# Latent up projection of a hybrid encoder layer: rotary parts of two neighbouring token tiles in one instruction each

## Chip, cores and metric

One core of a Trainium2 chip runs the whole layer. The metric is device microseconds (us) of one execution; the times given are medians of several runs. A profile is one further execution, recorded instruction by instruction. TensorE is called PE in the profile, VectorE DVE, ScalarE ACT, GpSimd POOL, and the queue that issues DMAs SP.

## The reference, cut to what matters

The layer has 1024 tokens of width 1024. After a modulated RMSNorm and an input projection it attends in two groups of eight heads: chunked attention (CA) and multi-head latent attention (MLA). Then come the output projection, and a gated feed-forward part. The change lies in the part that makes queries and keys of MLA out of the latents:

```python
q = jnp.dot(rmsnorm(q_lat, g_q_latent), w_q_up).reshape(B, S, 8, 96)
kv = jnp.dot(rmsnorm(kv_lat, g_kv_latent), w_kv_up).reshape(B, S, 8, 128)
k_nope, v = kv[..., :64], kv[..., 64:]
k = jnp.concatenate([k_nope, broadcast(k_rope[:, :, None, :], 8 heads)], axis=-1)
q = rmsnorm(q, g_mla_q); k = rmsnorm(k, g_mla_k)          # over the 96 numbers of a head
q = concat(q[..., :64], rope(q[..., 64:], positions))
k = concat(k[..., :64], rope(k[..., 64:], positions))
# rope(x): x1, x2 = the two halves of 16;  [x1*cos - x2*sin, x2*cos + x1*sin]
```

Each of a head's 96 numbers is thus 64 plain ones and 32 rotary ones. The rotary part of a key is the same for all eight heads, but for the factor that the norm puts on it.

## The kernel before, in words

Tokens are laid on the 128 partitions: eight token tiles of 128. Matrix products are made in three passes of fp32 values split into a high and a low part (`gemm3`, L154 to L156). Attention runs unit by unit (one head, one half of the queries): transposed pages of queries and keys (L697, with eviction and split at L705, L706, L709 and L710), scores (L771), the row minimum (L789, L790), the exponential (L797), its scaling and splitting into two fp16 parts (L799, L800, L73 on GpSimd, L819 on VectorE), a DMA transpose by SyncE's queue (L831), and the product with the values (L859), which is evicted at L868 and L869.

The projections that a later unit needs are written as generators, the *fillers* (`f_v`, `f_qk`, `f_m`, `f_up`, `f_oca`), from which `pace` draws pieces between the attention steps, so that their matmuls fill PE's gaps. The order of the program text is not the order on the engines: the framework schedules the whole layer as a list, by a simulated timeline of its own, and writes one fixed order for each engine. An engine works its list strictly in order, and waits with all that stands behind when an operand isn't there.

`f_up(gr)` (L596 to L659) makes queries, keys and values of four MLA heads, for `gr` 0 and 1. For each of the eight token tiles `t` it runs:

- six matmuls for the queries, evicted by ACT into `rq` (L632), which is one of four buffers of tag `R`; squares (L634) and their sums by head (L637, DVE);
- three matmuls for keys and values, the keys evicted into `raw` (L643, another buffer of tag `R`), their squares and sums (L645, L646, L647);
- `rsqrt_mean` on GpSimd (L119, L120): the factors `r`, four for the query heads and four for the key heads;
- the values (L650 on ACT, L651 on DVE);
- the queries: `q_t = rq * r` for all 96 numbers (L653), then `rope_apply` on the last 32 (L654), which is four DVE instructions, two products into the space of `rq` that is free by now (L465 with the cosines, L466 with the sines) and a difference and a sum of them (L467, L468);
- the keys: the plain 64 numbers times `r` (L657), and the rotary ones out of `kr`, where `f_m` has put them, times `r` (L658).

The query and key tiles `mq` and `mk` hold two token tiles each, [128, 2, 4, 96]. Their transposes (L697) need all four token tiles of a half. `f_up(0)` must be done before the first MLA unit, and its last tiles, and all of `f_up(1)`, run beside MLA attention. GpSimd has other work in that stretch: the low parts of the weights (L84) of `f_up(1)` (`wq`, `wk`) and of the output projection (`wo`), and of the transposed outputs (`cl`).

Of the kernel before, what the change touches and what calls it, by code (L numbers as in the profile page):

```python
# [13 lines left out]
F32 = mybir.dt.float32  # L14
# [8 lines left out]
MUL, ADD, SUB, MIN, MAX = ALU.mult, ALU.add, ALU.subtract, ALU.min, ALU.max  # L23

P = 128
# [8 lines left out]
QR, KVR, ROPE, NOPE, VD = 256, 128, 32, 64, 64  # L34
QK = NOPE + ROPE
# [29 lines left out]
def layer_kernel(ctx, tc, I, out):  # L65
    nc = tc.nc
    pe, act, dve, pool, sp = nc.tensor, nc.scalar, nc.vector, nc.gpsimd, nc.sync
# [7 lines left out]
    def hi_of(eng, o, i):  # L75
        if eng == "a":
            act.activation(o, i, AF.Copy)  # L77
        elif eng == "p":
            pool.tensor_scalar(o, i, 1.0, 0.0, op0=MUL, op1=ADD)
        else:  # L80
            dve.tensor_copy(o, i)

    def lo_of(eng, o, i, hi):
        (pool if eng == "p" else dve).tensor_tensor(o, i, f32(hi), op=SUB)  # L84

    cst = ctx.enter_context(tc.tile_pool(name="cst", bufs=1))
# [30 lines left out]
    def rsqrt_mean(r, ss, n, cols=None):  # L117
        sc = ss if cols is None else ss[:, cols]
        pool.tensor_scalar(sc, sc, 1.0 / n, EPS, op0=MUL, op1=ADD)  # L119
        anchor["r"] = pool.tensor_tensor(r, ss, nhalf[:].to_broadcast(list(r.shape)), op=ALU.pow).ins  # L120
# [8 lines left out]
    tabq = apg.tile([P, NT, 64], F32, name="tabq")  # L129
    tabk = apg.tile([P, NT, 64], F32, name="tabk")  # L130
    kr = apg.tile([P, NT, ROPE], F32, name="kr")
# [9 lines left out]
    def qtile(name):  # L141
        return apg.tile([P, 512], F32, name=name, tag="sq", bufs=2)
# [134 lines left out]
    for d in range(ND):  # L277
# [8 lines left out]
        for i in range(2):  # L286
            c0 = half * 256 + i * P
# [27 lines left out]
    def pow2_scale(nm, ssw, b2, n, fac):  # L315
        t = cst.tile([P, 3, ND], F32, name=f"vs{nm}")
        dve.tensor_tensor(t[:, 0, :n], ssw, b2, op=MUL)
        pt = ps.tile([P, 512], F32, name=f"vsp{nm}", tag="mm", bufs=2)
        pe.matmul(pt[:, :n], ones[:], t[:, 0, :n], start=True, stop=True)
        dve.tensor_reduce(t[:, 1, 0:1], pt[:, :n], axis=AX.X, op=ADD)  # L320
        dve.tensor_scalar(t[:, 1, 0:1], t[:, 1, 0:1], fac, 1e-30, op0=MUL, op1=ADD)
        pool.tensor_tensor(t[:, 1, 1:2], t[:, 1, 0:1], nhalf[:], op=ALU.pow)
        ab = cst.tile([P, 2], F32, name=f"vab{nm}")
        dve.tensor_scalar(t[:, 2, 0:1].bitcast(I32), t[:, 1, 1:2].bitcast(I32), 0x7F800000, None, op0=ALU.bitwise_and)
        dve.reciprocal(t[:, 2, 1:2], t[:, 2, 0:1])
        dve.tensor_scalar(t[:, 2, 1:2], t[:, 2, 1:2], 1.0001, None, op0=MUL)
        dve.tensor_scalar(t[:, 2, 1:2].bitcast(I32), t[:, 2, 1:2].bitcast(I32), 0x7F800000, None, op0=ALU.bitwise_and)
        dve.tensor_scalar(ab[:, 0:1], t[:, 2, 0:1], VSCALE, None, op0=MUL)
        dve.tensor_scalar(ab[:, 1:2], t[:, 2, 1:2], 1.0 / (VSCALE * PSCALE), None, op0=MUL)
        return ab[:, 0:1], ab[:, 1:2]  # L330
# [128 lines left out]
    def rope_apply(o, x, tab, t, nh, tmp, eng=pool):  # L459

        a = tmp[:, 0:nh * 32].rearrange("p (a b) -> p a b", a=nh)
        b = tmp[:, nh * 32:2 * nh * 32].rearrange("p (a b) -> p a b", a=nh)
        ct = tab[:, t:t + 1, 0:32].to_broadcast([P, nh, 32])
        sn = tab[:, t:t + 1, 32:64].to_broadcast([P, nh, 32])
        eng.tensor_tensor(a, x, ct, op=MUL)  # L465
        eng.tensor_tensor(b, x, sn, op=MUL)  # L466
        eng.tensor_tensor(o[:, :, 0:16], a[:, :, 0:16], b[:, :, 16:32], op=SUB)  # L467
        eng.tensor_tensor(o[:, :, 16:32], a[:, :, 16:32], b[:, :, 0:16], op=ADD)  # L468
# [119 lines left out]
    def g4(shape, dt, name):  # L588
        return G["4"].tile(shape, dt, name=name, tag="G4", bufs=8)
# [4 lines left out]
    mq, mk, mv = {}, {}, {}  # L594

    def f_up(gr):  # L596
        if gr == 0:
            right.__exit__(None, None, None)
            for i in "4v3":
                G["cm" + i] = tc.tile_pool(name="gp" + i, bufs=1, side="right", reuse_waits="tile")  # L600
                G[i] = G["cm" + i].__enter__()
        wq = []
        for k in range(2):
            raw = qtile(f"wqr{gr}_{k}")
            sp.dma_start(raw[:, :384], I["w_qu"][gr][:, k, :])
            w = g4([P, 2, 512], F32R, f"wq{gr}_{k}")
            hi_of("a", w[:, 0, :384], raw[:, :384])
            lo_of("p", w[:, 1, :384], raw[:, :384], w[:, 0, :384])
            wq.append(w)
        raw = qtile(f"wkr{gr}")  # L610
        sp.dma_start(raw[:], I["w_kvu"][gr])
        ssw = cst.tile([P, 1], F32, name=f"sswm{gr}")
        junk = qtile(f"wkj{gr}")
        act.activation(junk[:, 0:256].rearrange("p (a b) -> p a b", a=4),
                       raw[:].rearrange("p (a b) -> p a b", a=4)[:, :, NOPE:], AF.Square, accum_out=ssw[:])
        vscale["m", gr] = pow2_scale(f"m{gr}", ssw[:], gb2[:], 1, float(KVR))
        sc = vscale["m", gr][0]
        wk = g4([P, 2, 512], F32R, f"wk{gr}")
        hi_of("a", wk[:, 0], raw[:])
        lo_of("p", wk[:, 1], raw[:], wk[:, 0])  # L620
        for t in range(NT):
            h, j = divmod(t, 4)
            sl = slice(j * P, (j + 1) * P)
            if t % 2 == 0:
                mq[gr, t // 2] = g3([P, 2, 4, QK], F32, f"qn{gr}_{t}")
                mk[gr, t // 2] = g3([P, 2, 4, QK], F32, f"kn{gr}_{t}")
                mv[gr, t // 2] = G["v"].tile([P, 2, 4, 2, 64], F16, name=f"vt{gr}_{t}", tag="Gv", bufs=8)
            pt = ps.tile([P, 512], F32, name=f"qu{gr}_{t}", tag="mm", bufs=2)
            yield from gemm3_f(pt[:, :384], [(latT[k, h][:, 0, sl], latT[k, h][:, 1, sl], wq[k][:, 0, :384], wq[k][:, 1, :384])
                                for k in range(2)])  # L630
            rq = rtile(f"uqr{gr}_{t}")
            act.activation(rq[:, :384], pt[:, :384], AF.Copy)  # L632
            sq = qtile(f"usq{gr}_{t}")
            act.activation(sq[:, :384], rq[:, :384], AF.Square)  # L634
            ss = cst.tile([P, 8], F32, name=f"uss{gr}_{t}", tag="ss", bufs=4)
            r = cst.tile([P, 8], F32, name=f"ur{gr}_{t}", tag="rr", bufs=4)
            dve.tensor_reduce(ss[:, 0:4], sq[:, :384].rearrange("p (a b) -> p a b", a=4), axis=AX.X, op=ADD)  # L637
            pt = ps.tile([P, 512], F32, name=f"ku{gr}_{t}", tag="mm", bufs=2)
            yield from gemm3_f(pt[:], [(latT[2, h][:, 0, sl], latT[2, h][:, 1, sl], wk[:, 0], wk[:, 1])])
            p4 = pt[:].rearrange("p (a b) -> p a b", a=4)  # L640
            raw = rtile(f"kraw{gr}_{t}")
            r3 = raw[:, :256].rearrange("p (a b) -> p a b", a=4)
            act.activation(r3, p4[:, :, 0:NOPE], AF.Copy)  # L643
            s3 = raw[:, 256:512].rearrange("p (a b) -> p a b", a=4)
            act.activation(s3, r3, AF.Square)  # L645
            dve.tensor_reduce(ss[:, 4:8], s3, axis=AX.X, op=ADD)  # L646
            dve.tensor_tensor(ss[:, 4:8], ss[:, 4:8], ssr[:, t:t + 1].to_broadcast([P, 4]), op=ADD)  # L647
            rsqrt_mean(r[:], ss[:], QK)
            v_t = mv[gr, t // 2][:, t % 2]
            act.activation(v_t[:, :, 0, :], p4[:, :, NOPE:], AF.Copy, scale=sc)  # L650
            dve.scalar_tensor_tensor(v_t[:, :, 1, :], p4[:, :, NOPE:], sc, v_t[:, :, 0, :], op0=MUL, op1=SUB)  # L651
            q_t = mq[gr, t // 2][:, t % 2]
            dve.tensor_tensor(q_t, rq[:, :384].rearrange("p (a b) -> p a b", a=4),  # L653
                              r[:, 0:4].unsqueeze(2).to_broadcast([P, 4, QK]), op=MUL)  # L654
            rope_apply(q_t[:, :, NOPE:], q_t[:, :, NOPE:], tabq, t, 4, rq[:, 0:256], dve)
            k_t = mk[gr, t // 2][:, t % 2]
            dve.tensor_tensor(k_t[:, :, 0:NOPE], r3, r[:, 4:8].unsqueeze(2).to_broadcast([P, 4, NOPE]), op=MUL)  # L657
            dve.tensor_tensor(k_t[:, :, NOPE:], kr[:, t:t + 1, :].to_broadcast([P, 4, ROPE]),  # L658
                              r[:, 4:8].unsqueeze(2).to_broadcast([P, 4, ROPE]), op=MUL)  # L659


    def load_wo(k0, n, he, le):
# [541 lines left out]
    c0 = mt("c", [P, 4, 512], "c0")  # L1204
# [321 lines left out]
    for t in range(4):  # L1526
        o = dl.tile([P, 512], F32, name=f"oe{t}", tag="oe", bufs=3)
# [78 lines left out]
```

## Time and profile before

| What | us |
|---|---|
| median of 3 runs | 1341.02 (1340.53 to 1343.16) |
| the profiled execution, its own time | 1345.89 |
| its span, from the first to the last instruction | 1344.1 |
| PE busy | 1223.8 (91%) |
| DVE busy | 1096.2 (82%) |
| ACT busy | 622.7 (46%) |
| POOL busy | 578.1 (43%) |

In time, the layer is: modulation and the first projections, CA attention with the projections as fillers (to about 366 us), `f_up(0)` and the start of MLA (to about 396), MLA attention with `f_up(1)` beside it (to about 490), MLA attention with the first half of the output projection as its filler (to about 620), the other half of the output projection, and the feed-forward part to the end.

A row of the timeline gives the start of an instruction, its duration, the engine, the line, the operation, its operands and, in brackets, how long the engine had been idle before it. Durations of instructions that follow each other on VectorE overlap: the next one starts before the one ahead of it ends. So what an instruction takes of the engine is read from the distance between two starts, not from its duration. In a row of the waits the first name waited for the second; then come the total in us, the times, and the longest. A row of the windows gives the length of the stretch, the busy us of PE, PEld (weight loads), DVE, ACT and POOL, each with its instructions in brackets, TensorE's granted clock, and the DMA share.

### The profile page before, as it was taken

To read this page: it belongs to the slowest core of one execution; us is meant where nothing else is said; L and a number is where in the kernel's file an instruction comes from. 1 tells how busy PE (TensorE), PEld (TensorE's weight loads), DVE (VectorE), ACT (ScalarE), POOL (GpSimd) and SP (SyncE) were. 2 spreads that over 40 slices of the span, in tenths; PEclk is the share of its full clock that TensorE was granted. 3 is DMA by queue.
4 is the path that set the end of the run, shared out by engine and by line. 5 is a ranking of instruction groups with operands and counts; after the bars stand their busy time and mean duration, and the time that the engine had idled before them with its cause. 6 is when DMAs were issued, how large, how long until landed. Compare 5 with 4: busy or idle time off the path is not lost.

```text
span 1344.1 us, 18696 instructions
## 1 busy us (share of the span) xinstructions
PE 1223.8 (91%) x6168; PEld 1003.8 (75%) x6168; DVE 1096.2 (82%) x1928; ACT 622.7 (46%) x1132; POOL 578.1 (43%) x610
## 2 busy tenths in 40 slices
PE   4899798998877798886998999999999998999998
PEld 3788587896655567765776888888888886888886
DVE  6978798864679987894989988988899997687667
ACT  4453546443555544563376444444434444433431
POOL 5464557565646763354634444444445431000000
PEclk9899798998787889996999999999999998999999
DMA  8415577854413477779911333333323326943441
GB/s 323 138 35 116 135 177 179 192 127 110 87 32 80 94 153 165 141 150 252 377 49 47 126 110 133 103 122 98 133 102 118 126 98 241 390 141 117 130 161 63
DMA packets 223689, 190.57 MB, mean 142 GB/s; under 512 B 148708, under 2 KB 166884, under 8 KB 223592
## 3 DMA queue, kind: packets, MB, share of 16 engines
q1 hardware_dynamic: 223592, 189.38, 49.1%
q8 instruction: 48, 0.79, 0.2%
q14 instruction: 49, 0.40, 0.1%
HBM read 117.24 MB, written 37.49 MB: 115 GB/s over the span
## 4 chain that ended last, share of the span: by engine, by line
PE 41%; DVE 10%; issue 3%; ACT 2%; DMA 1%; POOL 1%; SPq 0%; DVEq 0%; ACTq 0%; POOLq 0%
PE p L1082 7%; PE p L1084 7%; PE p L1083 7%; PE dnA_P L1417 2%; PE dnA_P L1419 2%; PE dnA_P L1418 2%; PE dnB_P L1419 1%; PE dnB_P L1418 1%; PE dnB_P L1417 1%; DVE u L1253 1%; DVE u L1254 1%; PE op L154 1%; PE dnA L1417 1%; PE dnA L1419 1%; PE dnA L1418 1%
## 5 line engine op out<-in xcount | busy, mean ns | idle before, releaser
L77 ACT ACTIVATE dnP<-dnr 128x1024 fp32r<-128x1024 f32 x73 | 77.5, 1064 | 117.5 <-PE dnA_P L1419 46.4
L1391 DVE TENSOR_TENSOR dnP<-dnr,dnP 128x1024 fp32r<-128x1024 f32 x72 | 87.9, 1223 | 52.6 <-ACT dnP L77 52.6
L73 POOL TENSOR_SCALAR hlm<-Pm,rim 128x512 f16<-128x512 f32 (+3 forms) x96 | 68.8, 726 | 83.5 <-DVE rim L800 22.3
L84 POOL TENSOR_TENSOR wf<-wu,wf 128x512 fp32r<-128x512 f32 x22 | 38.8, 1762 | 116.3 <-ACT wf L77 116.3
L1253 DVE SCALAR_TENSOR_TENSOR u<-c,cvp,u 128x1023 f32<-128x1023 f32 x44 | 64.8, 1513 | 27.8 <-ACT u L1252 27.8
L73 POOL TENSOR_SCALAR hlc<-Pc,ric 128x640 f16<-128x640 f32 (+2 forms) x64 | 50.8, 797 | 61.0 <-ACT Pc L797 20.8
L819 DVE SCALAR_TENSOR_TENSOR hlm<-Pm,rim,hlm 128x512 f16<-128x512 f32 (+3 forms) x96 | 68.0, 719 | 9.8 <-POOL hlm L73 9.7
L797 ACT ACTIVATE Pc<-sc,mc 128x640 f32<-128x640 f32 (+2 forms) x64 | 42.1, 658 | 53.1 <-DVE mc L786 35.9
L797 ACT ACTIVATE Pm<-sm,mm 128x128 f32<-128x128 f32 (+3 forms) x64 | 47.1, 736 | 41.7 <-DVE mm L790 24.2
L84 POOL TENSOR_TENSOR wb<-wu,wb 128x512 fp32r<-128x512 f32 x22 | 38.1, 1732 | 64.5 <-ACT wb L77 50.7
L1252 ACT ACTIVATE u<-c,cvp 128x1024 f32<-128x1024 f32 x44 | 52.3, 1237 | 27.8 <-DVE c L1351 19.2
L1254 DVE SCALAR_TENSOR_TENSOR u<-c,cvp,u 128x1022 f32<-128x1022 f32 x44 | 63.8, 1488 | 0.0
L859 PE MATMUL pvm<-PTm,vt 128*128 128x256 f16 (+1 forms) x320 | 45.7, 294 | 17.0 <-DMA PTm<-hlm 9.9
L819 DVE SCALAR_TENSOR_TENSOR hlc<-Pc,ric,hlc 128x640 f16<-128x640 f32 (+2 forms) x64 | 51.6, 809 | 9.3 <-POOL hlc L73 8.7
L155 PE MATMUL ipq<-wq_s,hT 128*128 128x256 f32 x192 | 56.0, 292 | 0.1
L859 PEld LDWEIGHTS <-vt 128*128 128x128 f16 x320 | 31.6, 109 | 32.7 <-DMA PTm<-hlm 15.0
L154 PE MATMUL ipq<-wq_s,hT 128*128 128x256 f32 x192 | 55.8, 293 | 0.0
L156 PE MATMUL ipq<-wq_s,hT 128*128 128x256 f32 x192 | 55.4, 289 | 0.0
L77 ACT ACTIVATE wc<-ws 128x512 fp32r<-128x512 f32 x21 | 13.3, 632 | 88.0 <-DVE ws L1101 82.2
L1418 PE MATMUL dnA_P<-dnP 128*128 128x512 f32 x132 | 51.4, 389 | 0.0
L1419 PE MATMUL dnA_P<-dnP 128*128 128x512 f32 x132 | 51.3, 389 | 0.0
L1417 PE MATMUL dnA_P<-dnP 128*128 128x512 f32 x132 | 51.2, 389 | 0.0
(442 smaller groups left out, 4428.4 us busy)
## 6 DMA issues: line engine op xcount, KB each, us to landing
wu<-w_up SPq DMA_DIRECT2D x44, 512.0 KB, 3.5
dnr<-g_d SPq DMA_DIRECT2D x73, 256.0 KB, 2.8
aw<-w_ada SPq DMA_DIRECT2D x48, 256.0 KB, 3.5
g_d<-u SPq DMA_DIRECT2D x22, 512.0 KB, 3.0
dnr<-w_down SPq DMA_DIRECT2D x44, 256.0 KB, 5.3
adaw<-w_ada_a SPq DMA_DIRECT2D x16, 512.0 KB, 6.3
x<-x SPq DMA_DIRECT2D x16, 512.0 KB, 9.0
g_d<-gs SPq DMA_DIRECT2D x22, 256.0 KB, 2.8
```

The costliest lines, as they stand in the source:

```text
L73: pool.tensor_scalar(o, i, s, 1.0, op0=MUL, op1=MUL)
L77: act.activation(o, i, AF.Copy)
L797: act.activation(pr[:, :n], sv, AF.Exp, bias=m[:], scale=-1.0, accum_out=rsum[:, 0:1])
L819: dve.scalar_tensor_tensor(hl[:, w:2 * w], pp, ri[:], hl[:, :w], op0=MUL, op1=SUB)
L1082: pe.matmul(pt, sh, pg[:, 0], start=(k == 0 and not add), stop=False, skip_group_check=skip)
L1083: pe.matmul(pt, sh, pg[:, 1], start=False, stop=False, skip_group_check=skip)
L1084: last = pe.matmul(pt, sl, pg[:, 0], start=False, stop=(k == 3), skip_group_check=skip)
L1253: dve.scalar_tensor_tensor(u[:, 1:], c[:, :S - 1], cvp[:, cv + 1:cv + 2], u[:, 1:], op0=MUL, op1=ADD)
L1391: r = f(*a, **k)
L1417: pe.matmul(pt, sh, w[:, 0, 0], start=start, stop=False, skip_group_check=add)
L1418: pe.matmul(pt, sh, w[:, 1, 0], start=False, stop=False, skip_group_check=add)
L1419: pe.matmul(pt, sl, w[:, 0, 0], start=False, stop=stop, skip_group_check=add)
```

## The change

The factors of two neighbouring token tiles go into one tile, `rp` [128, 2, 8], two buffers instead of four single ones. In an even token tile the rotary work is left out; in the odd one it is done for both, by instructions that are twice as long: four for the queries instead of eight, one for the keys instead of two. The products with the cosines and sines now fill all 512 columns of the odd tile's `rq`; the `rq` of the even tile is read for the last time by its `q_t`.

```diff
-            r = cst.tile([P, 8], F32, name=f"ur{gr}_{t}", tag="rr", bufs=4)
+            if t % 2 == 0:
+                rp = cst.tile([P, 2, 8], F32, name=f"ur{gr}_{t}", tag="rp", bufs=2)
+            r = rp[:, t % 2]
...
-            rsqrt_mean(r[:], ss[:], QK)
+            rsqrt_mean(r, ss[:], QK)
...
-            rope_apply(q_t[:, :, NOPE:], q_t[:, :, NOPE:], tabq, t, 4, rq[:, 0:256], dve)
+            if t % 2:
+                x = mq[gr, t // 2][:, :, :, NOPE:]
+                a = rq[:, 0:256].rearrange("p (t a b) -> p t a b", t=2, a=4)
+                b = rq[:, 256:512].rearrange("p (t a b) -> p t a b", t=2, a=4)
+                for o, c0 in ((a, 0), (b, 32)):
+                    dve.tensor_tensor(o, x, tabq[:, t - 1:t + 1, c0:c0 + 32].unsqueeze(2).to_broadcast([P, 2, 4, 32]), op=MUL)
+                dve.tensor_tensor(x[:, :, :, 0:16], a[:, :, :, 0:16], b[:, :, :, 16:32], op=SUB)
+                dve.tensor_tensor(x[:, :, :, 16:32], a[:, :, :, 16:32], b[:, :, :, 0:16], op=ADD)
             k_t = mk[gr, t // 2][:, t % 2]
             dve.tensor_tensor(k_t[:, :, 0:NOPE], r3, r[:, 4:8].unsqueeze(2).to_broadcast([P, 4, NOPE]), op=MUL)
-            dve.tensor_tensor(k_t[:, :, NOPE:], kr[:, t:t + 1, :].to_broadcast([P, 4, ROPE]),
-                              r[:, 4:8].unsqueeze(2).to_broadcast([P, 4, ROPE]), op=MUL)
+            if t % 2:
+                dve.tensor_tensor(mk[gr, t // 2][:, :, :, NOPE:], kr[:, t - 1:t + 1, :].unsqueeze(2).to_broadcast([P, 2, 4, ROPE]),
+                                  rp[:, :, 4:8].unsqueeze(3).to_broadcast([P, 2, 4, ROPE]), op=MUL)
```

The code is moved by ten lines behind the change. In the changed kernel the products of the rotary part stand at L662, the difference and sum at L663 and L664, the keys' rotary part at L668, `q_t` at L655 and the keys' plain part at L666.

## The prediction

> **What bounds the kernel now.** First the page: which engine is full. Then the windows of the stretch that holds the changed lines, then the waits in it, then VectorE's timeline.
>
> ```profile
> span 1344.1 us, 18696 instructions
> ...
> PE 1223.8 (91%) x6168; PEld 1003.8 (75%) x6168; DVE 1096.2 (82%) x1928; ACT 622.7 (46%) x1132; POOL 578.1 (43%) x610
> ```
>
> The shares are means over stages; the changed lines run in one of them only, between 376 and 490 us. By stage:
>
> ```profile
> 376.00:396.00 20.00, 15.32 (x59) 11.38 (x57) 17.63 (x58) 11.15 (x28) 10.83 (x12) 0.83 0.03 7
> 396.00:490.00 94.00, 69.14 (x326) 53.06 (x325) 87.94 (x257) 53.53 (x125) 64.39 (x64) 0.78 0.44 96
> 490.00:620.00 130.00, 113.75 (x656) 89.72 (x655) 107.65 (x268) 67.33 (x140) 59.38 (x78) 0.97 0.75 158
> ```
>
> From 396 to 490 VectorE (the third pair) is busy 87.94 of 94 us, 94%, and PE 74%: here VectorE is the bound. From 490 to 620 PE is busy 87% and VectorE 83%; they wait for each other. From 376 to 396 VectorE has 88%, and the waits say what runs there. The first three rows are of 376 to 396, the next two of VectorE from 396 to 490, the last two of VectorE from 490 to 620:
>
> ```profile
> POOL uss L119 <- DVE uss L647: 14.3, 6, 5.6
> ACT uqr L632 <- DVE kn L657: 5.6, 4, 1.8
> DVE vt L651 <- ACT vt L650: 1.1, 1, 1.1
> ```
> ```profile
> DVE vt L651 <- ACT vt L650: 1.8, 3, 0.9
> DVE mk L710 <- ACT mk L709: 1.6, 1, 1.6
> ```
> ```profile
> DVE hlm L819 <- POOL hlm L73: 8.2, 14, 1.0
> DVE sm L789 <- PE sm L771: 6.3, 10, 1.1
> ```
>
> Up to 396 it is a loop: GpSimd waits for the sum of squares, VectorE for the factors that GpSimd makes of it, ACT for a buffer that VectorE's L657 frees. A shorter VectorE instruction helps there only if it stands on that loop. From 396 to 490 VectorE's waits are small, and time taken out of its list is time gained.
>
> **The change part by part.** Five of ten rotary instructions per pair of tiles go: 5 x 8 pairs = 40 of VectorE's 1928. One tile's block, undisturbed, in the timeline:
>
> ```profile
> 378.24 0.55 DVE L653 TENSOR_TENSOR qn<-uqr,ur 128x384 f32<-128x384 f32 x1
> 378.70 0.42 DVE L657 TENSOR_TENSOR kn<-kraw,ur 128x256 f32<-128x256 f32 x1
> 379.04 0.28 DVE L658 TENSOR_TENSOR kn<-kr,ur 128x128 f32<-128x128 f32 x1
> 379.25 0.28 DVE L465 TENSOR_TENSOR uqr<-qn,tabq 128x128 f32<-128x128 f32 x1
> 379.45 0.28 DVE L466 TENSOR_TENSOR uqr<-qn,tabq 128x128 f32<-128x128 f32 x1
> 379.76 0.22 DVE L467 TENSOR_TENSOR qn<-uqr 128x64 f32<-128x64 f32 x1
> 379.91 0.22 DVE L468 TENSOR_TENSOR qn<-uqr 128x64 f32<-128x64 f32 x1
> ```
>
> From start to start, 384 columns take 0.46 us, 256 take 0.34, 128 take 0.205, 64 take 0.15: about 1 ns per column and 0.075 us for the instruction. L467 comes 0.31 behind L466 and not 0.205: it reads what L466 wrote and waits 0.11 for it. So a tile's rotary work costs 0.21 + 0.20 + 0.31 + 0.15 + 0.15 = 1.02 us, a pair's 2.04. After: keys 0.34, products 0.34 and 0.34 + 0.11, difference and sum 0.205 each: 1.54. **Saved: 0.50 us per pair.** Columns are the same; what goes is five fixed costs (0.37) and one wait (0.11). That the new forms have one dimension more I price at nothing: L657, with a repeated operand of four heads, keeps the line of the others.
>
> How much of it is on the path? The groups from 366 to 490 us, and where L465 runs (five before 396, eleven behind):
>
> ```profile
> L653 DVE TENSOR_TENSOR qn<-uqr,ur 128x384 f32<-128x384 f32 x16 | 11.1, 692 | 0.2
> L657 DVE TENSOR_TENSOR kn<-kraw,ur 128x256 f32<-128x256 f32 x16 | 9.2, 573 | 0.0
> ...
> L465 DVE TENSOR_TENSOR uqr<-qn,tabq 128x128 f32<-128x128 f32 x16 | 4.9, 304 | 0.0
> L468 DVE TENSOR_TENSOR qn<-uqr 128x64 f32<-128x64 f32 x16 | 4.7, 296 | 0.0
> L658 DVE TENSOR_TENSOR kn<-kr,ur 128x128 f32<-128x128 f32 x16 | 4.6, 285 | 0.0
> L466 DVE TENSOR_TENSOR uqr<-qn,tabq 128x128 f32<-128x128 f32 x16 | 4.4, 277 | 0.0
> L467 DVE TENSOR_TENSOR qn<-uqr 128x64 f32<-128x64 f32 x16 | 4.3, 271 | 0.1
> ```
> ```profile
> 366.00:396.00 30.00, 1.41 (x5) 0.00 (x0) 0.77 0.21 38
> 396.00:490.00 94.00, 3.45 (x11) 0.00 (x0) 0.78 0.44 96
> ```
>
> - *Behind 396* (11 tiles, 5.5 pairs): 5.5 x 0.50 = **2.7 us**, on the bound engine. Ends: 0.37 per pair where something else stands between L466 and L467 anyway (2.0), and by durations instead of starts 2 x (3 x 0.28 + 2 x 0.22) - (3 x 0.42 + 2 x 0.28) = 0.74 per pair (4.1).
> - *Before 396* (2.5 pairs): between +1.25 saved and 1.5 lost, because in the built order the pair's block (1.54 us) stands in one piece ahead of the next tile's sum, for which GpSimd waits. I take 0: the loop waits, not VectorE.
> - *The even tile's buffer of tag R* is free after L653 and not after the rotary work; the row of ACT's waits names L657, which remains for the other buffer. 0, at best 0.3 per tile in the loop.
> - *The two factors in one tile* add no wait: in the built program each reader waits for its own tile's factors, and GpSimd's second write for none of VectorE's reads. 0.
> - *The first transposes of an MLA head* (L697) wait for both tiles of a pair. The last of the first half comes up to 0.5 us later (half a block), beside VectorE work that is to be done anyway. 0; if it isn't covered, 0.5.
> - *The order.* The scheduler lists all engines anew from 378 us to the end of attention, SP's queue included. Up to there the orders are the same; from the feed-forward part on too. It takes no instruction away; its price is bounded by the rivals.
>
> The sum is 2.7 us less than the profiled execution (1345.89 us, span 1344.1), so 1343.2 for such a one. That execution is 4.9 us above the median of the runs, 1341.0; the saving is in a stretch that both have: **1338.3**.
>
> [...]
>
> **The rivals.**
>
> *More hits between VectorE and GpSimd (slower).* In this stretch some VectorE instructions last about 1.05 us longer than their columns need, always beside a low part (L84) on GpSimd. First VectorE, then GpSimd:
>
> ```profile
> 408.43 1.63 DVE L653 TENSOR_TENSOR qn<-uqr,ur 128x384 f32<-128x384 f32 x1
> 409.98 1.50 DVE L657 TENSOR_TENSOR kn<-kraw,ur 128x256 f32<-128x256 f32 x1
> ...
> 412.18 1.17 DVE L467 TENSOR_TENSOR qn<-uqr 128x64 f32<-128x64 f32 x1
> 413.28 1.30 DVE L468 TENSOR_TENSOR qn<-uqr 128x64 f32<-128x64 f32 x1
> ```
> ```profile
> 408.36 1.28 POOL L84 TENSOR_TENSOR wk<-wkr,wk 128x512 fp32r<-128x512 f32 x1
> 409.60 1.60 POOL L84 TENSOR_TENSOR wo<-wor,wo 128x512 fp32r<-128x512 f32 x1
> ...
> 411.87 2.62 POOL L84 TENSOR_TENSOR wo<-wor,wo 128x512 fp32r<-128x512 f32 x2
> ```
>
> 1.63 against 0.55, 1.50 against 0.42, 1.17 and 1.30 against 0.22: 1.08, 1.08, 0.95 and 1.08 us. Over the groups above it is 16 x (0.14 + 0.15 + 0.02 + 0.08 + 0.05) = 7 us, about seven hits. In the built order seven two-input instructions stand together on VectorE, just behind the factors of tile 7: its L655 and L666, and for tiles 6 and 7 L668, L662 twice, L663 and L664. GpSimd's list has `wq`, `wk`, one scaling and five `wo` in a row at the same place. If each finds a low part ahead of it, there are seven hits where the rows have four, and as many again may come beside the three `wo` of 463 to 470 us. Six more hits cost 6.3 us: 1341.0 - 2.7 + 6.3 = **1344.6**. It decides from 2.5 hits more (no gain), and makes the kernel slower by 0.2% from five. For it speaks the block without a break; against it that two-input instructions become fewer, and that the five `wo` may come when VectorE reads PSUM.
>
> [...]
>
> *The gain is eaten (no change).* The loop gives 1.5 us back, and PE, at 87% from 490 to 620, waits for transposes that come when they came: 1341.0 - 2.7 + 1.5 + 1.2 = **1341**. For it speaks that 5 of 16 tiles stand in the loop; against it that VectorE has nearly no idle time behind.
>
> *More gain.* An instruction costs its duration's fixed part (8 x 0.74 = 5.9 us), or the new order takes away three hits beside the 2.7 (5.9): **1335.1**. For it: rotary instructions took 16 x (0.02 + 0.08 + 0.05) = 2.4 us of the hits. Against it: the starts.
>
> *The change doesn't do what it says*: excluded by the built program, which has the 40 instructions less.
>
> **How the numbers follow.** 0.2%, about what a measurement of this kernel can tell from no change, is 2.7 us: below 1338.3 is faster, above 1343.7 slower. The forecast, 1338.3 with 1337 to 1340, has 0.38, half of it faster, half within. No change (1341): 0.13, all within. More hits (1344.6): 0.29, all slower. More gain (1335.1): 0.20, all faster. So faster 0.39, same 0.32, slower 0.29. The range goes from 1333 (5.9 and two hits less) to 1346.5 (eight more hits); beyond it I leave 0.1 on each side at most. The likeliest case's own range is 1337 to 1340.
>
> **What would show it.** In the profile after: L662 with 0.34 us, L663 and L664 with 0.205 from start to start; rotary and key lines together about 4 us less busy, hits aside; VectorE at 94% or more in the 91 us behind 396, and the first `oc` matmuls 2 to 3 us earlier. Means of L655 and L666 above 692 and 573 ns speak for more hits. If the stretch to 490 is shorter and the end of attention isn't, the gain was eaten. The forecast is wrong if a start distance of L662 is above 0.45 us, or if the loop before 396 has grown by more than 1.5 us.

## The result, and the profile after

| | before | after |
|---|---|---|
| median of 4 runs, us | 1341.36 (1340.53 to 1343.16) | 1358.03 (1354.72 to 1358.3) |
| ratio, with its 95% interval | | 1.0114 (1.0095 to 1.0133) |
| the profiled execution's own time, us | 1345.89 | 1358.3 |
| its span, us | 1344.1 | 1356.5 |

The kernel became slower by 1.1%, some 15 us (the medians lie 16.7 us apart). The forecast was 1338.3, the range ended at 1346.5. The two profiled executions are 12.4 us apart, since that of before lay 4.5 us above its median; single runs of before went from 1337 to 1347 in the experiments below, so a difference of a few us between two traces is no finding by itself.

The page of after, to be held against the first lines of the prediction:

```profile
span 1356.5 us, 18659 instructions
...
PE 1228.1 (91%) x6168; PEld 1007.2 (74%) x6168; DVE 1099.2 (81%) x1888; ACT 622.8 (46%) x1132; POOL 574.7 (42%) x610
```

VectorE has its 40 instructions less (1888 for 1928), and is busy 3.0 us longer all the same. The windows of after, with the columns of before's:

```profile
376.00:396.00 20.00, 13.41 (x54) 9.58 (x53) 15.79 (x43) 12.03 (x30) 10.11 (x10) 0.91 0.03 7
396.00:490.00 94.00, 65.16 (x303) 49.85 (x302) 83.07 (x221) 51.30 (x119) 62.26 (x61) 0.75 0.42 88
490.00:620.00 130.00, 118.13 (x667) 93.29 (x666) 109.94 (x270) 67.28 (x141) 57.04 (x77) 0.96 0.78 152
```

In the stretch where VectorE was the fullest engine, from 396 to 490, it is now busy 83.07 of 94 us, 88% and not 94%, and PE does 4 us less there. Work that isn't done there is done later: from 490 to 620 both are busier than before. So the first question is why VectorE waits. Its waits from 385 to 455 us, after and then before:

```profile
DVE qn L655 <- POOL ur L120: 4.2, 5, 1.6
DVE uss L639 <- ACT usq L634: 3.7, 2, 2.9
...
```
```profile
DVE vt L651 <- ACT vt L650: 2.9, 4, 1.1
DVE mk L710 <- ACT mk L709: 1.6, 1, 1.6
```

The columns are the wait's sum, its count and the longest. Two stand out: 4.2 us for GpSimd's factors, which before's list doesn't have, and 3.7 for the squares of a tile (0.3 in before), 2.9 of them in one piece. For that piece the timelines of VectorE, PE and GpSimd in after are laid beside each other:

```profile
409.22 1.35 DVE L655 TENSOR_TENSOR qn<-uqr,ur 128x384 f32<-128x384 f32 x1 [0.49 <-POOL ur L120]
410.49 1.49 DVE L666 TENSOR_TENSOR kn<-kraw,ur 128x256 f32<-128x256 f32 x1
...
412.23 2.12 DVE L662 TENSOR_TENSOR uqr<-qn,tabq 128x256 f32<-128x256 f32 x2
414.39 1.23 DVE L663 TENSOR_TENSOR qn<-uqr 128x128 f32<-128x128 f32 x1
415.54 1.34 DVE L664 TENSOR_TENSOR qn<-uqr 128x128 f32<-128x128 f32 x1
...
416.88 1.54 DVE L829 SCALAR_TENSOR_TENSOR hlm<-Pm,rim,hlm 128x384 f16<-128x384 f32 x1
...
418.42 1.15 DVE L317 TENSOR_TENSOR vsm<-sswm,gb 128x1 f32<-128x1 f32 x1
...
423.50 0.55 DVE L639 TENSOR_REDUCE uss<-usq 128x4 f32<-128x384 f32 x1 [2.92 <-ACT usq L634]
```
```profile
416.94 0.66 PE L707 MATMUL mq_ps<-ident,qn 128*96 128x128 f32 x2 [4.98 <-DVE qn L664]
419.62 0.58 PE L319 MATMUL vspm<-vsm,ones 128*128 128x1 f32 x2 [2.01 <-DVE vsm L317]
420.06 0.67 PE L154 MATMUL qu<-wq,latT 128*128 128x384 f32 x1
```
```profile
412.65 6.90 POOL L84 TENSOR_TENSOR wo<-wor,wo 128x512 fp32r<-128x512 f32 x5
```

L317 is the first instruction of `pow2_scale`, the scale of the values of the second weight group, `f_up(1)`. In after it stands on VectorE behind the whole rotary block of the last tile of `f_up(0)`. On PE the scale's matmul (L319) stands ahead of the first matmul of `f_up(1)` (L154, `qu`), so that one starts at 420.06, though GpSimd was done with the last low part of its `wq` at 410.14, and VectorE, which has the last tile behind it, finds nothing to do: 2.92 us. Before, PE had this order:

```profile
406.92 0.45 PE L697 MATMUL mq_ps<-ident,qn 128*96 128x128 f32 x1 [2.44 <-DVE qn L468]
407.43 0.58 PE L319 MATMUL vspm<-vsm,ones 128*128 128x1 f32 x2
407.88 0.67 PE L154 MATMUL qu<-wq,latT 128*128 128x384 f32 x1
```

The same matmul ran at 407.88, beside the last tile's rotary block, and the next group's work was ready when that block ended. L317 is not the only instruction of this chain that stands further back in after. What it reads, the sum of squares of the weights, is made by ACT in L614, first in after and then in before:

```profile
412.96 0.40 ACT L614 ACTIVATE wkj<-wkr 128x256 f32<-128x256 f32 x1
```
```profile
405.98 0.42 ACT L614 ACTIVATE wkj<-wkr 128x256 f32<-128x256 f32 x1 [2.98 <-DMA wkr<-w_kvu]
```

So with L317 alone moved forward, the scale could not have started ahead of 413 us.

The second place is the output projection. SP's queue in after, and in before:

```profile
637.11 2.61 SPq L1127 DMA_DIRECT2D pa<-part_d  x4
640.22 0.46 SPq L881 DMA_DIRECT2D oT_d<-om  x1
647.89 0.81 SPq L1131 DMA_DIRECT2D x<-x  x2
```
```profile
630.07 0.46 SPq L871 DMA_DIRECT2D oT_d<-om  x1
630.57 0.59 SPq L1117 DMA_DIRECT2D pa<-part_d  x1
631.20 0.90 SPq L1121 DMA_DIRECT2D x<-x  x2
```

In after 7.7 us lie between the store of the last attention output and the load of `x`. The chain of waits says what fills them:

```profile
640.22 7.66 DMA oT_d<-om
```

The load of `x` waits until the store has landed: in the built program it waits for the semaphore that this store raises. Nothing in the data asks for that; the memory does. The output tile of the last unit takes one of the four buffers of tag `R`. In after's list it gets the one at byte 40896 of each partition, which ends at 42944, and the first tile of `x` lies from 42624. In before it got the one at 38720, which ends at 40768, and `x` lay from 42496. Which of the four it gets follows from the order.

### The profile page after: what moved, and what is told of

The parts are those of the page before. It is cut to its first block, busy times and chain, and to the rows that moved or that the text cites. A ratio compares the mean times of both kernels' runs of the same rounds, so it can differ in the third digit from the quotient of the medians.

```text
span 1356.5 us, 18659 instructions
## 1 busy us (share of the span) xinstructions
PE 1228.1 (91%) x6168; PEld 1007.2 (74%) x6168; DVE 1099.2 (81%) x1888; ACT 622.8 (46%) x1132; POOL 574.7 (42%) x610
## 4 chain that ended last, share of the span: by engine, by line
PE 42%; DVE 10%; issue 3%; DMA 3%; ACT 2%; POOL 1%; SPq 0%; DVEq 0%; ACTq 0%; POOLq 0%
PE p L1093 7%; PE p L1094 7%; PE p L1092 7%; PE dnA_P L1427 2%; PE dnA_P L1428 2%; PE dnA_P L1429 2%; PE dnB_P L1428 1%; PE dnB_P L1427 1%; PE dnB_P L1429 1%; DVE u L1263 1%; DMA PTm<-hlm 1%; PE sm L781 1%; DVE u L1264 1%; DVE hlm L829 1%; PE pvm L869 1%
## 5 line engine op out<-in xcount | busy, mean ns | idle before, releaser
L869 PE MATMUL pvm<-PTm,vt 128*128 128x256 f16 (+1 forms) x320 | 48.9, 304 | 24.6 <-DMA PTm<-hlm 17.6
L869 PEld LDWEIGHTS <-vt 128*128 128x128 f16 x320 | 32.6, 112 | 42.4 <-issue 20.6
L154 PE MATMUL ipq<-wq_s,hT 128*128 128x256 f32 x192 | 56.6, 298 | 0.0
```

What stands on the lines that cost most here:

```text
L869: last = pe.matmul(dst, u.vst(j), mov, start=(x == 0), stop=(x == len(todo) - 1), skip_group_check=True)
```

## The experiments

Four theories. **1**: the order of the queues, which the framework lists anew, costs the time, and not the changed instructions. **2**: the pairing itself costs: longer two-input instructions beside GpSimd, and an even tile that is held until the odd one. **3**: the shared factor tile makes a tile wait for its neighbour. **4**: the loss lies in the order of the tiles ahead of 400 us. Every ratio below is against runs of before that were measured together with that kernel; their medians were 1341.84, 1341.46, 1343.67 and 1341.74 us in the four groups of experiments.

### The change in parts: rp_only, key_only, rope_only

`rp_only` keeps the lines of before but for the shared tile `rp`; `key_only` pairs L668 alone, `rope_only` L662 to L664 alone:

```diff
-            r = cst.tile([P, 8], F32, name=f"ur{gr}_{t}", tag="rr", bufs=4)
+            if t % 2 == 0:
+                rp = cst.tile([P, 2, 8], F32, name=f"ur{gr}_{t}", tag="rp", bufs=2)
+            r = rp[:, t % 2]
...
-            rsqrt_mean(r[:], ss[:], QK)
+            rsqrt_mean(r, ss[:], QK)
```

> The kernel before with one part of the change alone: the factors r of two neighbouring tiles lie in one tile of two buffers; every rotary part is made per tile as before. All engines have the instructions of before in the order of before, and SBUF from this tile on is shifted by 128 bytes for everything alike. Theory 1 (the loss of 16.7 us comes from the order of the queues after the list is made anew, at three places: about 5 us near 410 to 422 us, about 3.5 us near 530 to 541, about 3.6 us in the output projection): the order is that of before, so the time is that of before, 1341.4 us, within 0.2%. Theory 2 (the pairing itself costs: longer two-input instructions bunched in the odd tile, and the even tile held until it): 1341.4 too. Theory 3 (the shared factor tile makes a tile wait for its neighbour): a loss of several us, 1345 or more.

> The change for the keys alone: the rotary part of the keys is made for two tiles in one instruction in the odd tile; the rotary part of the queries stays per tile. On VectorE the scale of the second weight group stands ahead of the last tile's rotary part, as in before, and the last output tile's buffer doesn't overlap the first tile of x. Theory 1 (order): neither the loss of about 5 us near 420 us nor that of 3.6 us in the output projection; the rest of the order is new, so 1341 give or take 4 us, 1337 to 1346. Theory 2 (pairing itself): one instruction of five is paired, so a fifth of 16.7 us, 1344.7, and with it longer instructions in the odd tile.

> The change for the queries alone: their rotary part is made for two tiles at once in the odd tile; the key's rotary part stays per tile. On VectorE the scale of the second weight group stands behind the last tile's rotary part, as in after; the last output tile's buffer doesn't overlap the first tile of x, as in before. Theory 1 (order): the loss of about 5 us near 420 us is there, that of 3.6 us in the output projection is not: 1346 to 1352, with the first matmul of the second weight group near 420 us and not near 408. Theory 2 (pairing itself): four instructions of five are paired, so four fifths of 16.7 us, 1354.8.

Measured: `rp_only` 1339.45, ratio 0.9982 (0.9969 to 0.9996); `key_only` 1345.78, 1.0032 (1.0016 to 1.0048); `rope_only` 1345.44, 1.0036 (1.0013 to 1.0058). `rp_only` has the order of before on every engine. Theory 3 falls. That `rp_only` comes out 0.18% faster, with 1 outside its interval, though its lists are those of before, says that differences below 0.2% shouldn't be read as more than that. The two halves lose 0.3% each. `key_only` fits both theories (1337 to 1346, and 1344.7) within about 1 us, `rope_only` neither: theory 1 gave it 1346 to 1352, theory 2 gave it 1354.8. In `rope_only` the first matmul of the second group came at 418.15, as theory 1 had it, and VectorE waited 2.7 us for that tile's squares; in `key_only` it came at 407.06, and `x` isn't overlapped either. So `key_only` loses its 0.3% in another way. Both halves have an order of their own, so these runs can't separate instructions from order.

### Instructions against order: a_in_b_order, b_in_a_order

Here the order is written down. For each engine the kernel holds a list of all its instructions, and edges that fix the issue order alone:

```diff
         layer_kernel(ctx, tc, I, out)
+        L=nc.cur_bb.bb.instructions
+        by={i.name: i for i in L}
+        nosync=mybir.DependencyInfo(mybir.DependencyClass.NoSync, mybir.DependencyReason.DATA)
+        for o in ORDER:
+            for a, b in zip(o, o[1:]):
+                tc.add_manual_dep(by[f"I-{b}"], f"I-{a}", nosync, reason="order")
```

> The instructions of after, in the order of before: on each engine every instruction is held behind the one that stands ahead of it in before's list. The paired instructions stand where the odd tile's stood, and on TensorE the transposes of an even tile of the first pages stand right ahead of those of its odd tile (four instructions in 6128 change place). Theory 1 (the loss comes from the order alone): the paired instructions then bring what they save on VectorE, some 2 to 3 us: 1337 to 1341. Theory 2 (the pairing itself costs: longer two-input instructions beside GpSimd, the even tile held until the odd one): the loss stays, 1350 or more. Between the two, 1343 to 1348, both would hold in part.

> The mirror of it: the instructions of before, none of them paired, in the order of after; the even tile's five rotary instructions, which after doesn't have, stand behind that tile's scaling of queries and keys. Its last output tile lies over the first tile of x, as in after. Theory 1 (order alone): as slow as after or slower by what the pairing saves, 1356 to 1362. Theory 2 (pairing itself): the time of before, about 1342.

Measured: after's instructions in before's order 1341.98, ratio 1.0000 (0.9979 to 1.0022); before's instructions in after's order 1355.80, ratio 1.0102 (1.0074 to 1.0131). This decides it: **the order alone makes the loss, and without it the pairing costs nothing** that these runs resolve (0.2%). It saves nothing that they resolve, either: both times lie just outside what theory 1 gave (1337 to 1341, and 1356 to 1362). VectorE's waits from 385 to 455 us go with the order too, those of `a_in_b_order` first, then those of `b_in_a_order`:

```profile
DVE mk L720 <- ACT mk L719: 1.6, 1, 1.6
DVE qn L655 <- POOL ur L120: 1.0, 2, 0.8
```
```profile
DVE uss L637 <- ACT usq L634: 2.9, 1, 2.9
...
DVE qn L653 <- POOL ur L120: 2.2, 4, 0.8
```

The piece of 2.9 us is there with per-tile instructions and gone with paired ones. So is the late load of `x`, in SP's queue of `b_in_a_order`:

```profile
635.13 0.46 SPq L871 DMA_DIRECT2D oT_d<-om  x1
644.00 0.81 SPq L1121 DMA_DIRECT2D x<-x  x2
```

### The late load of x: om_pg, b_overlap

Two kernels move the last output tile to other buffers. In `om_pg` (after) it leaves the place where `x` lies, in `b_overlap` (before) it is put there:

```diff
-                    dst = rtile(f"o{u.nm}_{u.g}") if final else \
+                    dst = pgtile([P, 512], F32, f"o{u.nm}_{u.g}") if final else \
```
```diff
-                    dst = rtile(f"o{u.nm}_{u.g}") if final else \
+                    dst = qtile(f"o{u.nm}_{u.g}") if final else \
```

> The kernel after, with the last output tile of the attention in a buffer of another group (that of the wide score tiles), which the first tile of x doesn't overlap; all engines have the instructions of after in the order of after. So the load of that tile of x on SP no longer waits until the store of the last output tile has landed (640.2 to 647.9 us in after). Theory 1 (three places): the loads of x go out some 7 us earlier, and about 3.6 us of the 16.7 come back: 1354.4. Theory 2 (pairing itself, or the two-input instructions slowed beside GpSimd): this wait is hidden, 1358.0 within 0.2%.

> The kernel before with one word changed: the attention's last output tile lies in the buffers of the squares, which the first tile of x lies over. The order of before stays up to the end of the attention (some 20 of 10222 instructions change place around it, among them one store of a finished part on SP). If the wait of the load of x for the store of the last output tile costs what it cost in after, 3.1 us by the traces (51.3 us against 48.2 from the first to the last matmul of the output projection) and up to 6.5 by the medians (1358.0 against 1351.5): 1344.5 to 1348. If that difference was the spread of the runs: 1342.

Measured: `om_pg` 1351.51, ratio 1.0075 (1.0057 to 1.0092), where after has 1.0114; `b_overlap` 1347.38, ratio 1.0024 (1.0009 to 1.0038). SP's queue, first of `om_pg`, then of `b_overlap`:

```profile
637.50 0.46 SPq L881 DMA_DIRECT2D oT_d<-om  x1
638.00 1.17 SPq L1131 DMA_DIRECT2D x<-x  x2
```
```profile
630.06 0.46 SPq L871 DMA_DIRECT2D oT_d<-om  x1
638.56 0.81 SPq L1121 DMA_DIRECT2D x<-x  x2
```

Where the two tiles don't overlap, `x` follows the store after half a microsecond; where they do, after 8.5. The price is 0.24% from the one side and 0.39% from the other, 3 to 5 us, each known to about 0.2%. Theory 2 would have left `om_pg` at 1358; theory 1 gave it 1354.4, so more came back than I expected. In `om_pg` the lists are those of after; in `b_overlap` some 20 instructions around the end of the attention stand otherwise, among them a store on SP's queue, so its figure holds them too.

### Where in the order: split_1, split_2, rsplit_1, split_05

The lists of `om_pg` and of `a_in_b_order` are spliced: the first up to a point and the second behind it, or the other way round in `rsplit_1`. The instructions are those of `om_pg`, paired. In the table, `a_in_b_order` has the same instructions, but for the place of the last output tile, which doesn't lie over `x` there either.

> The instructions of after with the last output tile in the buffer group that x doesn't overlap (that kernel took 1351.5), in the order of after up to the low part of the second page of the first head (near 419 us), and from there in the order of before. Theory 1a (what is lost by 420 us, with VectorE short of work while the second weight group's first tile is late, is never regained): 1345 to 1348. Theory 1b (that loss is regained, the end comes from the order behind it): 1342 or less. If the pairing costs by itself it is 1350 or more.

> The same, but in the order of after up to the first matmul of the attention's output part (near 487 us), and from there in the order of before. Theory 1a: the whole loss up to there, 1345 to 1348, and what the order of the last 130 us of the attention adds (some 5 us between 500 and 540 in the traces) is missing, so clearly below the 1351.5 of the whole order. Theory 1b: 1342 or less, and all of the loss lies in the order of the attention behind 487 us.

> The instructions of after with the last output tile in the other buffer group (1351.5), in the order of before up to the low part of the second page of the first head (near 412 us there), and from there in the order of after: the reverse of the first splice. Theory 1 (what the order of after loses besides the late loads of x is lost by about 419 us, in the stretch of the sixth and seventh tile): the time of before, ratio within 0.3% of 1.000. If the order behind it, the attention's 200 us, loses by itself: a ratio of 1.005 or more.

> The same instructions in the order of after up to the scaling of the last tile's queries (near 409 us), and from there in that of before, so with the scale of the second weight group and its first tile ahead of the last tile's rotary part and with the low parts of the output weights as in before. Theory 1a (the loss lies behind 409 us: the late first tile of the second group, beside the low parts in a row): ratio within 0.2% of 1.000. Theory 1c (half of it is already lost from 398 to 409 us, where the last tile comes later): 1.003 to 1.005.

| after's order | ratio | interval |
|---|---|---|
| nowhere (`a_in_b_order`) | 1.0000 | 0.9979 to 1.0022 |
| up to 409 us (`split_05`) | 1.0042 | 1.0024 to 1.0060 |
| up to 419 us (`split_1`) | 1.0059 | 1.0038 to 1.0079 |
| up to 487 us (`split_2`) | 1.0064 | 1.0049 to 1.0079 |
| from 412 us (`rsplit_1`) | 1.0033 | 1.0019 to 1.0047 |
| everywhere (`om_pg`) | 1.0075 | 1.0057 to 1.0092 |

By 419 us most of the loss of `om_pg` is made, and it isn't regained: theory 1a holds against 1b in the first two, though with 1350.6 and 1350.7 us both lie above the 1345 to 1348 that I expected, and `split_2` not clearly below `om_pg`. I had put 1350 or more down to the pairing itself; `a_in_b_order`, with the same instructions, rules that out. `split_05` falls to theory 1c (1.003 to 1.005): something is lost ahead of 409 us already. Its row is less firm than the interval says, since its ten runs went from 1343 to 1353 us. `rsplit_1` lies between its two numbers, at the edge of the first one (within 0.3% of 1.000). If all of the loss lay between 409 and 419 us, both would have lost nothing. The loss is not in one place; and a splice has a seam, at which two lists that weren't made for each other meet, so the rows don't add up to the last one exactly.

### The scale of the second group: scale_up, scale_down, scale_early

`scale_up` is `om_pg` with some 23 instructions moved forward in its lists, the scale (L614 on ACT too) and the first tile of `f_up(1)`. `scale_down` is before with the same ones moved back. `scale_early` is an edit of the source of after, with a new list by the framework:

```diff
-        raw = qtile(f"wkr{gr}")
-        sp.dma_start(raw[:], I["w_kvu"][gr])
...
+        for g2 in ((1, 0) if gr == 0 else (1,)):
+            raw = qtile(f"wkr{gr}_{g2}")
+            sp.dma_start(raw[:], I["w_kvu"][g2])
+            if gr == 0:
...
+                vscale["m", g2] = pow2_scale(f"m{g2}", ssw[:], gb2[:], 1, float(KVR))
```

> The kernel of after with the last output tile in the other buffer group (1351.5), in the order of after but for the scale of the second weight group and that group's first tile, which are moved up: on ScalarE the sum of squares stands ahead of the cast of the key weights, on VectorE the scale's first instruction stands behind the scaling of the last tile's queries and not behind its rotary part, on TensorE the scale's matmul and the nine of the first tile stand ahead of the last tile's transposes, on GpSimd its power ahead of the five low parts of the output weights. Some 23 of 10182 instructions move. Theory 1 (VectorE runs out of work near 420 us because this first tile is late): VectorE's idle time between 385 and 455 us falls from 11.8 us to some 6, and 5 to 7 us come back: 1344.5 to 1346.5. Theory 4 (the loss by 419 us lies in the order of the tiles ahead of it, 376 to 400 us): within 2 us of 1351.5.

> The mirror: the instructions of before in the order of before, and only the scale of the second weight group and that group's first tile stand as far back as in after: behind the last tile's rotary part on VectorE, behind its transposes on TensorE, behind the low parts of the output weights on GpSimd. Nothing is paired. Theory 1: VectorE idles near 420 us as in after, and 5 to 7 us are lost: 1346.5 to 1348.5. Theory 4: within 2 us of before, 1342.

> The kernel after with one edit of the source, and its order listed anew by the framework: the scales of both weight groups are made ahead of the first group's tiles (the second group's key weights are loaded once more for it, 256 KB); the last output tile doesn't overlap the first tile of x. Theory 1: neither the idle VectorE near 420 us nor the late loads of x; whatever else the new order brings, some 4 us either way around before: 1338 to 1346. If the pairing cost by itself: 1350 or more.

Measured: `scale_up` 1348.91, ratio 1.0036 (1.0022 to 1.0050) against `om_pg`'s 1.0075; `scale_down` 1346.54, ratio 1.0027 (1.0014 to 1.0040); `scale_early` 1353.91, ratio 1.0074 (1.0056 to 1.0091).

Moving the scale and the first tile gives 0.39% back in the one kernel and takes 0.27% in the other: 3.6 to 5.2 us, at the lower end of what I expected or below it. Theory 4, which gave nothing to either, falls as an account of the whole; as one of a part it doesn't, since `split_05` loses 0.42% with after's order up to 409 us only. PE in `scale_up`, then PE and VectorE's largest wait in `scale_down`:

```profile
411.85 0.67 PE L154 MATMUL qu<-wq,latT 128*128 128x384 f32 x1
```
```profile
413.79 0.67 PE L154 MATMUL qu<-wq,latT 128*128 128x384 f32 x1
```
```profile
DVE uss L637 <- ACT usq L634: 3.3, 1, 3.3
```

In `scale_up` the first tile comes 8 us earlier than the 420.06 of after, and VectorE's wait for squares falls from 3.7 us (in `om_pg`) to 2.0. In `scale_down` it comes 6 us later than the 407.88 of before, and the wait comes with it. A part of my expectation failed, though: VectorE's idle time from 385 to 455 us didn't fall to 6 us in `scale_up`, it went from 11.8 to 13.5. Busy time was the wrong measure, since a VectorE instruction that is held up beside a low part on GpSimd counts as busy (in after L655 counts 1.35 us there, at 409.22, and 0.55 alone): in `scale_up` 168 instructions took 56.53 us, in `om_pg` 155 took 58.15. PE in the same 70 us tells it rightly, in the windows of `om_pg` and then of `scale_up`: 46.48 us of matmuls against 49.29, at a granted clock of 0.76 against 0.83.

```profile
385.00:455.00 70.00, 46.48 (x210) 35.37 (x209) 58.15 (x155) 38.11 (x92) 44.81 (x41) 0.76 0.28 64
```
```profile
385.00:455.00 70.00, 49.29 (x229) 37.69 (x228) 56.53 (x168) 39.48 (x95) 45.03 (x45) 0.83 0.29 65
```

`scale_early` is a plain miss. The scale is out of the way, but the new list puts the last tile's transposes behind its rotary block and ahead of other matmuls once more, with the `wo` low parts beside the block (413.13 to 420.07 on GpSimd). PE in `scale_early`:

```profile
418.99 0.66 PE L710 MATMUL mq_ps<-ident,qn 128*96 128x128 f32 x2 [4.55 <-DVE qn L667]
```

That is nearly the same idle PE as after's 4.98 us at 416.94. An edit of the source that takes one bad neighbour away lets the framework make another.

### What stays open

Of after's 1.14%, the late load of `x` takes 0.24 to 0.39%, the late scale and first tile 0.27 to 0.39%. If the two add up, which no run shows, 0.36 to 0.63% are left, and each of these figures is known to some 0.2%. This rest I can't put to one place: the splices have shares of it ahead of 409 us and behind 412 us, and `key_only` loses 0.3% without either place. The traces show one candidate, VectorE's wait for GpSimd's factors (4.2 us in after, 4.1 in `om_pg`, 1.0 in `a_in_b_order`, none listed in before); no run changed it by itself, and `b_in_a_order`, which loses nearly as much as after, has only 2.2 us of it. Nor is it separated how much of the loss goes through TensorE's granted clock: it was 0.942 to 0.949 in after's runs and 0.946 to 0.959 in those of before.

## Why the prediction was wrong, point by point

- **What bounds the kernel**: VectorE was the fullest engine from 396 to 490 us, as read. That time taken out of its list is time gained isn't shown: with the paired instructions in before's order no gain is measured (1.0000). Nor is idle time of VectorE there the measure of a loss: in `scale_up` it rose while the kernel became faster.
- **The saving of 0.50 us per pair** came as worked out, where nothing disturbs it. A pair's block in after:

```profile
390.43 0.55 DVE L655 TENSOR_TENSOR qn<-uqr,ur 128x384 f32<-128x384 f32 x1
390.89 0.42 DVE L666 TENSOR_TENSOR kn<-kraw,ur 128x256 f32<-128x256 f32 x1
391.23 0.42 DVE L668 TENSOR_TENSOR kn<-kr,ur 128x256 f32<-128x256 f32 x1
...
391.64 0.75 DVE L662 TENSOR_TENSOR uqr<-qn,tabq 128x256 f32<-128x256 f32 x2
392.42 0.29 DVE L663 TENSOR_TENSOR qn<-uqr 128x128 f32<-128x128 f32 x1
392.63 0.29 DVE L664 TENSOR_TENSOR qn<-uqr 128x128 f32<-128x128 f32 x1
```

  From start to start 0.33 for the keys, 0.78 for both products with the wait behind them, 0.21 for the difference and 0.21 for the sum: 1.53 us, where 1.54 was forecast. Whether the 2.7 us reach the end can't be told: `a_in_b_order` has them in its interval (0.9979 is -2.8 us) and has 0 in the middle of it, so the rival by which the gain is eaten fits it no worse.
- **The loop before 396, the buffers, the factor tile and the first transposes**, priced at 0 together: `a_in_b_order`, which holds them all and the saving too, shows 0 within 0.2%, and `rp_only` shows no loss for the shared tile. These steps held as far as the runs can see, to some 0.2%.
- **"The order ... takes no instruction away; its price is bounded by the rivals."** This step failed. The rivals bounded it with 6 us of one mechanism, and the new order cost 1.02% (`b_in_a_order`), some 14 us, with no instruction added. Of after's 1.14%, about half to two thirds went by two mechanisms that I had not looked for; the cause of the rest is open. The first: a short chain of another group (L614, L317), listed behind the block, with the next group's first matmul behind it on PE. I read the new list for VectorE's and GpSimd's neighbours and not for what PE could start. The second: a buffer's address, which follows from the order, laid an output tile over `x`. SP's list showed the load of `x` behind the store in both kernels; that it waits for the landing was to be read from the built program alone.
- **The rival of more hits** had the right side and the wrong mechanism. In the block it came as described: L655, L666, the second L662, L663 and L664 last 0.8 to 1.1 us longer, the first L662 0.3. But over the stretch the hits on these lines didn't grow; they moved from the first two to the rotary ones: from 366 to 490 us L662, L663 and L664 have means of 518, 417 and 432 ns against medians of 415, 283 and 280. L655 and L666 have means of 623 and 520 ns in after, where I had named 692 and 573 as the mark:

```profile
L655 DVE TENSOR_TENSOR qn<-uqr,ur 128x384 f32<-128x384 f32 x16 | 10.0, 623 | 4.9 <-POOL ur L120 4.7
L666 DVE TENSOR_TENSOR kn<-kraw,ur 128x256 f32<-128x256 f32 x16 | 8.3, 520 | 0.0
```

- **The marks** did their work. VectorE at 94% or more behind 396 was the one that failed first (88%), and it pointed at the waits and not at the instructions. The first `oc` matmul (output projection), forecast 2 to 3 us earlier, came at 486.86 after 486.69; at the attention's last eviction (L879, L869 in before) after's trace is 10 us behind, 639.43 after 629.28.
- **The range** was too narrow on the slow side, since it took the bounds of one mechanism for the bounds of the order. Of four kernels with a new list and an edit in this part (after, `key_only`, `rope_only`, `scale_early`) all four were slower than before, by 0.3 to 1.1%.

## What to carry to other kernels

Where a framework lists the order anew, price the list and not only the instructions: follow each chain that crosses the changed block, and ask for every engine what it can start while the block runs. Then look which buffers get other addresses, and whether a load now lies over a tile whose store is still on its way. To learn whether a loss is the edit's or the list's, run the new instructions in the old order and the old ones in the new order; two kernels settle what variants of the source, each with a list of its own, leave open.

## What the runs showed of the hardware

- In these rows a hit by a low part on GpSimd hardly depended on the width of the VectorE instruction. L317 works on one column, and beside the five `wo` of after it lasted 1.15 us (above), where before, with no low part beside it, it took 0.15; L655, with 384 columns, lasted 1.35 in after beside `wq` (409.15 to 410.14 on GpSimd) instead of 0.55. Not every VectorE instruction was hit: beside two `wo` of before (415.03 to 417.54) L637, with one input, lasted 0.54, and L706 and L651, which read one of their inputs from PSUM, 0.68 and 0.47; their medians from 366 to 490 us are 0.55, 0.67 and 0.48. Nor did every GpSimd instruction hit: the factors' L120, whose inputs lie in SBUF as those of a low part do, left these as short as elsewhere: L317's 0.15 us in before fell into it (406.75 to 408.39), and so did most of the undisturbed block that the prediction priced (378.24 to 380.13). So not every GpSimd instruction that reads SBUF held VectorE up for its whole length, as far as the starts and lengths of these rows go.

```profile
407.23 0.15 DVE L317 TENSOR_TENSOR vsm<-sswm,gb 128x1 f32<-128x1 f32 x1
```
```profile
378.93 1.69 POOL L120 TENSOR_TENSOR ur<-uss,nhalf 128x8 f32<-128x8 f32 x1
```

- In after a store of 128 KB took 7.66 us to land when it was issued behind four loads of 512 KB (640.22); the median of these stores from 480 to 640 us was 2.4.
